# A softmax with a relative position bias: another assignment of row blocks to partitions

## The chip, the cores and the metric

The kernel runs on one core of one Trainium2 chip. The metric is the time of one execution on the device in microseconds, median of the runs shown. Beside it stands a profile of one execution, with its own time and its span, which is the time from the first to the last instruction of the core.

## What is computed

`logits` has the shape 2 x 8 x 2112 x 2112 (batch, head, row, column) in float32, `rel_bias` 8 x 33. Each row gets a bias that depends only on head and on row minus column, clipped to -16..16, and is then put through a softmax:

```
rel = pos[:, None] - pos[None, :]
rel_clipped = np.clip(rel, -16, 16) + 16
logits = logits + rel_bias[:, rel_clipped][None]
logits = logits - logits.max(axis=-1, keepdims=True)
exp = np.exp(logits)
out = exp / exp.sum(axis=-1, keepdims=True)
```

The input and the output have 285.5 MB each; the output has the shape and type of `logits`.

## The kernel before

**Tiling.** There are 2 x 8 x 2112 = 33792 rows. They are cut into 128 blocks of RP = 264 neighbouring rows, and partition p holds block p, for the whole run. NB = 8 blocks make up one head of one batch, so the low three bits of p say which eighth of the 2112 rows the block is (q in the code), and the next three bits are the head (h). A block is walked in steps of R = 6 rows: one buffer `X[m]` holds 6 x 2112 float32, 50688 bytes, in each partition. There are NBUF = 4 buffers and K = 11 rounds over them, so 44 buffers in all.

**Data movement.** `rows` (line 71) gives the DRAM address pattern of one buffer: 128 runs of 50688 bytes, one for each partition, RP * S elements apart. `load` (line 88) issues it from SyncE (SP) and `store` (line 91) from ScalarE (ACT); each is one DMA of 6336 KB. Four loads are issued at the start; after that, SP waits for the store of buffer m (the wait is in `take`, line 86) and issues the load of the next round into it.

**Work on a buffer.** For each of the six rows of a buffer, VectorE (DVE) adds the bias to the logits, negates and takes the minimum in one custom instruction (`add`, line 184), then ACT takes exp with that minimum as its bias and sums the row (`exps`, line 195). When all six are done, DVE takes the reciprocals (line 208) and scales four of the rows (line 211); ACT scales the other two (line 216) and issues the store (line 93). The order on each engine is written out by hand, in two loops, one on DVE and one on ACT, and semaphores join them. An `add` waits for its load by the semaphore `ld[m]`, again in `take` at line 86, as all the waits do that also lower a semaphore.

**Setup.** Before the loops, each partition builds the vector `F` of the bias that its block of rows sees, from its own q and h. Pool writes the partition's number into `pid` (line 124). DVE cuts q and h out of it with an and and a shift (lines 131 and 132), copies both as floats into `qh` in PSUM (line 135), and compares them with 0, 1, 2 ... (line 140). A small DMA from ACT's queue (line 120) brings the table of biases; line 142 is the first that needs it. `settle` is a wait of DVE for its own earlier instructions. The loop copies the part of `F` that a round needs into `F2` (line 170).

```
def rows(t, k, m):
    return bass.AP(
        tensor=t.tensor, offset=t.offset + m * R * S + k * (G * S), ap=[[RP * S, P], [1, R * S]],
    )
```

Of the kernel before, what the change touches and what calls it, by code (L numbers as in the profile page):

```python
# [8 lines left out]
I32 = mybir.dt.int32  # L9
ACTF = mybir.ActivationFunctionType  # L10
ALU = mybir.AluOpType
# [4 lines left out]
def kernel(  # L16
# [6 lines left out]
    nc = tc.nc  # L23
    P = 128
    B, H, S, S2 = logits.shape
# [3 lines left out]
    RP = B * H * S // P  # L29
# [5 lines left out]
    R = 6  # L35
    G = NBUF * R
# [5 lines left out]
    io = ctx.enter_context(tc.tile_pool(name="io", bufs=1))  # L42
    X = [io.tile([P, R * S], FP32, tag=f"X{b}", name=f"X{b}") for b in range(NBUF)]
    F2 = io.tile([P, SW + 1], FP32, tag="F2", name="F2")
    pid = io.tile([P, 2], I32, tag="pid", name="pid")
    own = io.tile([P, W + 2 * NB + 1], FP32, tag="own", name="own")
    rbK, rest, reg = own[:, 0:W], own[:, W : W + NB], own[:, W + NB : W + 2 * NB + 1]
    nmax = io.tile([P, NBUF * R], FP32, tag="nmax", name="nmax")
# [8 lines left out]
    def small(n):  # L57
        zc[0] += 16 * -(-n // 16)
        return Z[:, zc[0] - 16 * -(-n // 16) : zc[0] - 16 * -(-n // 16) + n]

    eq, lt, hsel = (small(NB) for _ in range(3))
    le, gt = (small(NB + 1) for _ in range(2))
    qh = small(2)

    def view(t, offset, dims):
        return bass.AP(tensor=t.tensor, offset=t.offset + offset, ap=[[list(t.ap[0])[0], P]] + dims)

    def rows(t, k, m):
        return bass.AP(
            tensor=t.tensor, offset=t.offset + m * R * S + k * (G * S), ap=[[RP * S, P], [1, R * S]],  # L70
        )

    with tc.tile_critical(no_gpsimd_drain=True):  # L73
# [8 lines left out]
        idx = nc.alloc_semaphore("idx")  # L82
        dve = nc.alloc_semaphore("dve")

        def take(eng, sem, n):
            eng.wait_ge(sem, n).then_inc(sem, -n)  # L86

        def load(k, m):
            nc.sync.dma_start(out=X[m][:, :], in_=rows(logits, k, m)).then_inc(ld[m], 16)

        def store(k, m):
            take(nc.scalar, scaled, R)
            nc.scalar.dma_start(out=rows(out, k, m), in_=X[m][:, :]).then_inc(st[m], 16)
# [10 lines left out]
        v = nc.vector  # L104
        done = [0]

        def then(ins):
            done[0] += 1
            ins.then_inc(dve, 1)

        def settle():
            take(v, dve, done[0])
            done[0] = 0
# [7 lines left out]
            out=bass.AP(tensor=F2.tensor, offset=F2.offset, ap=[[Q * step, P // Q], [1, H * W]]),  # L121
            in_=bass.AP(tensor=rel_bias.tensor, offset=rel_bias.offset, ap=[[0, P // Q], [1, H * W]]),
        ).then_inc(rb, 16)
        nc.gpsimd.iota(pid[:, :], pattern=[[0, 2]], base=0, channel_multiplier=1).then_inc(idx, 1)
        nc.gpsimd.iota(
            num, pattern=[[1, NB + 1]], base=0, channel_multiplier=0,
            allow_small_or_imprecise_dtypes=True,
        ).then_inc(idx, 1)

        v.wait_ge(idx, 2)  # L130
        then(v.tensor_scalar(out=pid[:, 0:1], in0=pid[:, 0:1], scalar1=NB - 1, scalar2=None, op0=ALU.bitwise_and))
        then(v.tensor_scalar(out=pid[:, 1:2], in0=pid[:, 1:2], scalar1=3, scalar2=H - 1,
                             op0=ALU.logical_shift_right, op1=ALU.bitwise_and))
        settle()
        then(v.tensor_copy(out=qh, in_=pid[:, :]))
        settle()
        q, h = qh[:, 0:1], qh[:, 1:2]
        for o, n, s, op in ((eq, NB, q, ALU.is_equal), (lt, NB, q, ALU.is_lt), (hsel, NB, h, ALU.is_equal),
# [24 lines left out]
                           in_=view(reg, 1, [[1, NB - 1], [0, RP - W]])))  # L163
# [97 lines left out]
```

## Time and profile before

| what | value |
|---|---|
| median of 3 runs | 1325.65 us (1325.03 to 1326.21) |
| the profiled execution, its own time | 1327.36 us |
| its span | 1325.6 us |
| bytes read and written in HBM | 285.48 MB and 285.47 MB |
| mean rate of the DMA engines | 431 GB/s |
| DVE busy | 866.1 us |
| ACT busy | 757.2 us |
| load, issue to landing, median | 39.0 us |
| store, issue to landing, median | 58.8 us |

The profile has one line for each group of instructions: line of the kernel, engine, operation, tiles written and read, shape and count; then the busy time in us and the mean of one in ns; then the idle time of the engine just before these instructions and what ended it. "DVEq L86" is DVE's own queue at the wait in line 86. In the queue lines, q1 carries the loads from SP, q10 the stores (and the table of biases) from ACT, and the last number is the time of its packets as a share of 16 engines over the span. In the line of tenths, each digit is the busy share of one fortieth of the span.

### The profile page before, as it was taken

How to read it: one execution, taken by the hardware profiler on the slowest of the kernel's cores; microseconds unless marked ns; L12 is line 12 of the kernel's file. 1: busy time of each engine (PE TensorE's matmuls, PEld its weight loads, DVE VectorE, ACT ScalarE, POOL GpSimd, SP SyncE). 2: the span in 40 equal slices, each digit the busy share in tenths (PEclk: the TensorE clock that was granted, in tenths of full speed). 3: DMA queues.
4: the chain of work that ended last, by engine and by line, in shares of the span. 5: the costliest groups of instructions: out<-in, count | busy, mean ns of one | idle time of the engine just before them, and what ended most of it. 6: DMA issues, size and time to landing. Idle time of an engine off the chain costs nothing. (4 is left out here: it accounts for less than half of the span.)

```text
span 1325.6 us, 2109 instructions
## 1 busy us (share of the span) xinstructions
DVE 866.1 (65%) x781; ACT 757.2 (57%) x627; POOL 0.4 (0%) x6
## 2 busy tenths in 40 slices
DVE  6886656566766675566667566556766676566663
ACT  3776555556665565555556565555665665555563
POOL 0000000000000000000000000000000000000000
DMA  9999999999999999999999999999999999999998
GB/s 416 416 433 424 441 428 428 441 424 433 441 428 431 436 425 433 439 430 434 434 430 433 437 434 425 437 434 434 428 439 436 422 441 434 431 431 436 428 433 389
DMA packets 12682, 570.98 MB, mean 431 GB/s; under 512 B 1412, under 2 KB 1416, under 8 KB 1416
## 3 DMA queue, kind: packets, MB, share of 16 engines
q1 hardware_dynamic: 6336, 285.48, 50.1%
q10 hardware_dynamic: 6344, 285.48, 49.8%
q14 instruction: 2, 0.02, 0.0%
HBM read 285.48 MB, written 285.47 MB: 431 GB/s over the span
## 5 line engine op out<-in xcount | busy, mean ns | idle before, releaser
L195 ACT ACTIVATE X<-X,nmax 128x2112 f32<-128x2112 f32 x264 | 542.6, 2055 | 508.0 <-DVE nmax L184 475.3
L184 DVE CUSTOM_DVE_ANT_0 X<-X,F 128x2112 f32<-128x2112 f32 x264 | 605.2, 2354 | 322.3 <-DVEq L86 322.3
L211 DVE TENSOR_SCALAR X<-X,rec 128x2112 f32<-128x2112 f32 x176 | 220.3, 1315 | 2.8
L216 ACT ACTIVATE X<-X,rec 128x2112 f32<-128x2112 f32 x88 | 176.1, 2048 | 17.2 <-DVE rec L208 12.2
L208 DVE RECIPROCAL rec<-tot 128x6 f32<-128x6 f32 x44 | 8.4, 191 | 106.2 <-DVEq L86 106.2
L195 ACT ACTIVATION_READ_ACCUMULATOR X<-X,nmax 128x1 f32 x264 | 49.2, 186 | 0.0
L195 ACT ACT_TABLE_LOAD x11 | 14.1, 1283 | 22.6 <-ACTq L86 19.9
L170 DVE COPY F<-F 128x2135 f32 x11 | 26.1, 2373 | 0.5 <-DVEq L86 0.5
L184 DVE DVE_READ_ACCUMULATOR2_ANT nmax<- 128x1 f32 x264 | 21.7, 82 | 0.0
L142 DVE LOAD_MASK_SELECT F<-F x1 | 0.0, 14 | 6.0 <-DMA F<-in_rel_bias_dram 6.0
L162 DVE COPY F<-own 128x1617 f32<-128x1617 f32 x1 | 1.8, 1835 | 0.0
L118 DVE MEMSET F<- 128x264 f32 x1 | 0.3, 278 | 1.1 <-SPq L73 1.1
L140 DVE TENSOR_SCALAR Z<-rec,Z 128x8 f32<-128x8 f32 (+1 forms) x5 | 0.8, 227 | 0.1
L148 DVE TENSOR_REDUCE own<-F 128x33 f32<-128x264 f32 x1 | 0.6, 608 | 0.1
L161 DVE TENSOR_TENSOR F<-F,own 128x264 f32<-128x264 f32 x1 | 0.4, 442 | 0.1
L145 DVE TENSOR_TENSOR F<-F,Z 128x264 f32<-128x264 f32 x1 | 0.4, 428 | 0.1
L142 DVE STREAM_SHUFFLE F<-F 128x264 f32<-128x264 f32 x1 | 0.4, 443 | 0.0
L158 DVE TENSOR_TENSOR F<-Z,own 128x264 f32<-128x264 f32 x1 | 0.4, 432 | 0.0
L166 DVE COPY F<-own 128x247 f32<-128x247 f32 x1 | 0.4, 410 | 0.0
L164 DVE COPY F<-own 128x247 f32<-128x247 f32 x1 | 0.4, 408 | 0.0
L156 DVE SCALAR_TENSOR_TENSOR own<-Z,own 128x8 f32<-128x8 f32 x1 | 0.2, 227 | 0.2 <-DVEq L86 0.2
L153 DVE TENSOR_SCALAR own<-Z,own 128x8 f32<-128x8 f32 x1 | 0.2, 226 | 0.1
(11 smaller groups left out, 1.6 us busy)
## 6 DMA issues: line engine op xcount, KB each, us to landing
X<-in_logits_dram SPq DMA_DIRECT2D x44, 6336.0 KB, 39.0
out_dram<-X ACTq DMA_DIRECT2D x44, 6336.0 KB, 58.8
F<-in_rel_bias_dram ACTq DMA_DIRECT2D x1, 4.1 KB
```

Of the source, the lines that this page charges most:

```text
L140: then(v.tensor_scalar(out=o, in0=num[:, 0:n], scalar1=s, scalar2=None, op0=op))
L142: then(v.stream_shuffle(out=T, in_=T, mask=[0] * Q))
L145: then(v.tensor_tensor(out=heads, in0=view(F2, 0, [[W, H], [1, W]]), in1=view(hsel, 0, [[1, H], [0, W]]), op=ALU.mult))
L148: then(v.tensor_reduce(out=rbK, in_=view(F2, H * W, [[1, W], [W, H]]), axis=mybir.AxisListType.X, op=ALU.add))
L158: then(v.tensor_tensor(out=bands, in0=view(eq, 0, [[1, NB], [0, W]]), in1=view(rbK, W - 1, [[0, NB], [-1, W]]), op=ALU.mult))
L162: then(v.tensor_copy(out=view(F, C0 + W, [[RP, NB - 1], [1, RP - W]]), in_=view(reg, 1, [[1, NB - 1], [0, RP - W]])))
L170: then(v.tensor_copy(out=F2[:, 0:SW], in_=F[:, bass.ds(RP - G - k * G, SW)]))
L184: v.tensor_tensor_reduce(out=row(m, i), in0=row(m, i), in1=F2[:, x : x + S], scale=-1.0, scalar=BIG, op0=ALU.add, op1=ALU.min, accum_out=c ...
L195: nc.scalar.activation(out=row(m, i), in_=row(m, i), func=ACTF.Exp, scale=-1.0, bias=col(nmax, m, i), accum_out=col(tot, m, i),).then_inc( ...
L208: v.reciprocal(out=col(rec, m, 0, R), in_=col(tot, m, 0, R)).then_inc(inv, 1 if m < NBUF - 1 else NBUF + 1)
L211: v.tensor_scalar_mul(out=row(m, i), in0=row(m, i), scalar1=col(rec, m, i)).then_inc(scaled, 1)
L216: nc.scalar.activation(out=row(m, i), in_=row(m, i), func=ACTF.Copy, scale=col(rec, m, i),).then_inc(scaled, 1)
```

## The change

Partition p = 8e + j (e from 0 to 15, j from 0 to 7) holds block 16j + e in place of block 8e + j. The DRAM side of each load and store is written with two outer dimensions in place of one: 16 steps of one block, and in each of them 8 steps of 16 blocks. The order of the partitions in SBUF, the size of each run, the number of DMAs and both loops are unchanged.

Since a block's eighth and head follow from its number, the setup finds them in another way. With b = 16j + e, the eighth is q = e mod 8, which is (p >> 3) and 7, and the head is (b >> 3) mod 8 = (2j + (e >> 3)) mod 8, that is 2 (p and 3) + (p >> 6). `pid` gets a third column for it, and the sum is made in floats by one more instruction.

```
-    pid = io.tile([P, 2], I32, tag="pid", name="pid")
+    pid = io.tile([P, 3], I32, tag="pid", name="pid")
...
-    qh = small(2)
+    qh, qs = small(2), small(1)
...
+    E = 16
+
     def rows(t, k, m):
         return bass.AP(
-            tensor=t.tensor, offset=t.offset + m * R * S + k * (G * S), ap=[[RP * S, P], [1, R * S]],
+            tensor=t.tensor, offset=t.offset + m * R * S + k * (G * S),
+            ap=[[RP * S, E], [E * RP * S, P // E], [1, R * S]],
         )
...
-        nc.gpsimd.iota(pid[:, :], pattern=[[0, 2]], base=0, channel_multiplier=1).then_inc(idx, 1)
+        nc.gpsimd.iota(pid[:, :], pattern=[[0, 3]], base=0, channel_multiplier=1).then_inc(idx, 1)
...
+        then(v.tensor_scalar(out=pid[:, 0:1], in0=pid[:, 0:1], scalar1=3, scalar2=None, op0=ALU.logical_shift_right))
+        then(v.tensor_scalar(out=pid[:, 1:2], in0=pid[:, 1:2], scalar1=3, scalar2=1,
+                             op0=ALU.bitwise_and, op1=ALU.logical_shift_left))
+        settle()
+        then(v.tensor_scalar(out=pid[:, 2:3], in0=pid[:, 0:1], scalar1=3, scalar2=None, op0=ALU.logical_shift_right))
         then(v.tensor_scalar(out=pid[:, 0:1], in0=pid[:, 0:1], scalar1=NB - 1, scalar2=None, op0=ALU.bitwise_and))
-        then(v.tensor_scalar(out=pid[:, 1:2], in0=pid[:, 1:2], scalar1=3, scalar2=H - 1,
-                             op0=ALU.logical_shift_right, op1=ALU.bitwise_and))
-        settle()
-        then(v.tensor_copy(out=qh, in_=pid[:, :]))
+        settle()
+        then(v.tensor_copy(out=qh, in_=pid[:, 0:2]))
+        then(v.tensor_copy(out=qs, in_=pid[:, 2:3]))
+        settle()
+        then(v.tensor_scalar(out=qh[:, 1:2], in0=qh[:, 1:2], scalar1=qs, scalar2=None, op0=ALU.add))
         settle()
```

## Prediction

> **What bounds the kernel now.** I read the summary page first: the busy times, the DMA lines and the queues.
>
> ```profile
> span 1325.6 us, 2109 instructions
> ...
> DVE 866.1 (65%) x781; ACT 757.2 (57%) x627; POOL 0.4 (0%) x6
> ...
> DMA  9999999999999999999999999999999999999998
> GB/s 416 416 433 424 441 428 428 441 424 433 441 428 431 436 425 433 439 430 434 434 430 433 437 434 425 437 434 434 428 439 436 422 441 434 431 431 436 428 433 389
> DMA packets 12682, 570.98 MB, mean 431 GB/s; under 512 B 1412, under 2 KB 1416, under 8 KB 1416
> ...
> q1 hardware_dynamic: 6336, 285.48, 50.1%
> q10 hardware_dynamic: 6344, 285.48, 49.8%
> q14 instruction: 2, 0.02, 0.0%
> ```
>
> No compute engine is near full, while the DMA line is at nines throughout. The two queues together hold 50.1 + 49.8 = 99.9% of the time of the 16 DMA engines, so there is hardly a gap between two transfers on any engine. The packets are long: 12682 less 1416 small ones and 2 instruction fetches are 11264, which is 44 x 128 on each queue, one row of six rows of logits (6 x 2112 x 4 = 50688 bytes) for each partition. Each engine therefore carries 704 of them, 352 from each queue. A load packet takes 0.501 x 1325.6 / 352 = 1.887 us, a store packet 0.498 x 1325.6 / 352 = 1.875 us (completion writes included). So the time of this kernel is one number, **704 packets at 1.881 us on each engine, 1324.3 us**, plus 1.3 us around it. The profiled execution took 1327.36 us, 1.76 more than its span; the median shown, 1325.65, lies 1.71 below that, so that a time worked out for the span is also one for the median.
>
> Next I ask whether the compute engines could become the bound, from the groups of instructions.
>
> ```profile
> L195 ACT ACTIVATE X<-X,nmax 128x2112 f32<-128x2112 f32 x264 | 542.6, 2055 | 508.0 <-DVE nmax L184 475.3
> L184 DVE CUSTOM_DVE_ANT_0 X<-X,F 128x2112 f32<-128x2112 f32 x264 | 605.2, 2354 | 322.3 <-DVEq L86 322.3
> ```
>
> DVE idles 322.3 us at the wait of line 86, the one on the load's semaphore. That is the idle time that a late load causes; over 44 buffers it is 7.3 us for each. Slower DMA goes straight into the time, and faster DMA would have some 7 us of room in each 30.1 us (1324.3 / 44) before DVE became the bound.
>
> Then the stages, since a mean over the span could hide one: loads alone at the start, loads and stores in turn, stores alone at the end. Columns are the stretch, its length, the busy times, the clock, the DMA share and GB/s.
>
> ```profile
> 0.00:18.00 18.00, 9.11 (x23) 1.28 (x1) 0.43 (x6) 1.00 0.96 397
> 18.00:40.00 22.00, 18.88 (x17) 16.89 (x14) 0.00 (x0) 1.00 0.95 412
> ...
> 120.00:600.00 480.00, 312.08 (x275) 275.04 (x228) 0.00 (x0) 1.00 1.00 432
> 600.00:1200.00 600.00, 391.38 (x348) 344.75 (x287) 0.00 (x0) 1.00 1.00 433
> ...
> 1300.00:1325.60 25.60, 5.20 (x5) 4.56 (x4) 0.00 (x0) 1.00 0.86 374
> ```
>
> With loads alone the rate (412) is within 5% of that with both kinds (432 and 433). The packets take the same 1.88 us whether an engine's neighbours read or write. So in this kernel the 16 engines **never slow one another**: not in memory, and not where they enter the 128 partitions. The views of one line's DMAs give the same from the other side: the fastest load and the fastest store, the ones that run by themselves.
>
> ```profile
> DMA to landing us min/median/max: 17.5/39.0/82.6
> ```
>
> ```profile
> DMA to landing us min/median/max: 18.2/58.8/59.5
> ```
>
> Eight packets of 1.88 us are 15.0 us, so a lone load (17.5) and a lone store (18.2) have about 3 us of start and completion beside them.
>
> **The change part by part.** There are two parts: the setup on DVE and Pool that finds each partition's head and block, and the address pattern of the 88 large DMAs.
>
> *Setup.* The old chain on pid, from the timeline (start, length):
>
> ```profile
> 1.30 0.15 DVE L131 TENSOR_SCALAR pid<-pid 128x1 int32<-128x1 int32 x1
> 1.38 0.14 DVE L132 TENSOR_SCALAR pid<-pid 128x1 int32<-128x1 int32 x1
> 1.67 0.16 DVE L135 CAST Z<-pid 128x2 f32<-128x2 int32 x1
> 1.98 0.77 DVE L140 TENSOR_SCALAR Z<-rec,Z 128x8 f32<-128x8 f32 x5
> 8.74 0.01 DVE L142 LOAD_MASK_SELECT F<-F  x1 [5.99 <-DMA F<-in_rel_bias_dram]
> ```
>
> The change makes seven small instructions of these first three and adds two waits for DVE's own semaphore: four instructions at 0.16 us and two gaps of about 0.15 us (1.52 to 1.67 is one), 0.9 us. The iota of 3 columns in place of 2 adds nanoseconds. Behind it, line 142 waits 5.99 us for the bias table; the 0.9 us lie wholly inside. If that cover were gone, they would go into the first add, once: 0.9 us of 1325. I take 0. Everything after line 142 is unchanged in number and size, in both loops too.
>
> *The pattern.* Bytes, packet size and number of DMAs stay (128 runs of 50688 bytes, 44 loads, 44 stores). What moves is which block a partition holds, and the form in which the DRAM side is written: one dimension of 128 becomes 16 by 8. Two costs hang on this.
>
> The issue itself: SP and ACT write one instruction for each DMA; a second dimension may make each dearer.
>
> ```profile
> L89 SPq DMA_DIRECT2D X<-in_logits_dram x44: 332/333/631, 1.0 to 1246.0; - x44
> ...
> L93 ACTq DMA_DIRECT2D out_dram<-X x44: 338/338/380, 40.3 to 1306.3; - x44
> ```
>
> At 0.33 us each, even doubling them costs ACT 0.34 us per buffer, beside 475.3 / 44 = 10.8 us in which it waits for DVE. Behind the store on ACT's queue stand the next buffer's exps, which wait for DVE anyway. SP only waits for stores. I take 0; at the two ends, where nothing covers it, it is at most 0.63 us.
>
> The dealing out: 128 partitions are dealt to 16 engines, and before shows a dealing in which no two engines meet. The diff replaces it. [...] Nothing in the trace shows what this new dealing does, so its price is bounded from both sides. Below: the loads lose what they take longer than stores, 50.1 - 49.8 = 0.3% of 1325.6, **4.0 us**; a packet faster than a store's 1.875 us is seen nowhere, so no gain beyond. Above: if the engines meet in pairs at the same partitions' entrance, both at half rate, a packet takes 3.76 us, and the sum is 1325.6 + c x 1324.3, where c is the share of the work that an engine does while its mate is at the same place. c = 0 gives 1326, c = 1 gives 2650.
>
> [...]
>
> Which c? One instruction hands all 16 engines their rows at one moment and in one order, so mates are in step, and every DMA waits for the slowest of the 16, so a pair that runs ahead is stopped at the next semaphore. That speaks for the high end. Against it: loads and stores alternate on each engine, so a mate that is one packet off writes while the other reads, and if the two directions don't disturb each other this costs nothing. I take c between 0.5 (only one direction meets, 1988 us) and 1 (2650 us), the middle, 0.75: 1325.6 + 993.2 = **2320 us**, nearer to the upper end because nothing in the loop brings mates out of step.
>
> **The rivals.**
>
> *Forecast, slower by meeting in pairs:* 2320, with 1500 (c = 0.13) to 2680 (c = 1 and one buffer's 30.1 us exposed) as its own bounds.
>
> *No effect:* the order in which blocks are visited doesn't matter, because 99.9% of the engines' time is streaming at one rate; or the change doesn't do what it says, and the chip deals the 16 by 8 pattern as before. For it: the flat rate in all stages. Against: then the dealing would have to be blind to the form. 1325.7 us.
>
> *Faster:* loads lose their 4.0 us because neighbouring blocks suit the memory better: 1321.6 us (-0.3%). For it: loads take 1.887 to the stores' 1.875 us, so there is something to lose. Against: part of this is the cold first load (397 GB/s in the first 18 us), which stays, and the engines must not meet. It decides only if more than 2.7 of the 4.0 us go and no pair meets.
>
> *Slightly slower by memory:* the 16 streams, now one block (264 x 2112 x 4 = 2.23 MB) apart, meet in DRAM. The lowest rate of a full slice on the page is 416 against 431: 431/416 x 1325.6 = 1373 us. It decides once the memory gives less than the engines' 431 GB/s; against it, no stage shows memory as a limit.
>
> **How the numbers follow.** Chances: forecast 0.78, slightly slower 0.06, no effect 0.10, faster 0.06. The rows weigh so because the gain is capped at 0.3% by a full DMA line, while the loss has no such cap and the one thing that keeps it away, the dealing without meetings, is what the diff rewrites. [...] About 0.2% (2.7 us) is what a measurement of this kernel can tell from no change. Faster by more than that: 0.06. Within: 0.10. Slower: 0.78 + 0.06 = 0.84. The range takes in the forecast's bounds and reaches down to the slight loss, 1370 to 2680; what is left out is no effect, faster, and a sliver beyond the bounds, together 0.2.
>
> **What would show it.** In the changed kernel's page, the packets (12682) and MB should be the same and the queues' shares still near 100% together, but with about 246 GB/s (571 MB / 2320 us) and packets of 3.3 us. The lone load and the lone store are the sharpest test: 17.5 and 18.2 us become 25 to 33 if mates meet, and stay if not. DVE's wait at the load's semaphore should grow from 7.3 us a buffer to about 30; DVE's and ACT's busy times stay at 866 and 757. If the load-only stage is slow and the mixed one is not, mates are out of step and c is near 0; if only loads are slow, one direction meets. I am wrong if the lone load lands in 17 to 18 us: then engines don't meet, and the time is within 4 us of 1325.

## The result, and the profile after

The changed kernel takes 1789.28 us, median of 6 runs (1746.99 to 1858.69), where the kernel before took 1325.86 us (1325.03 to 1328.78). The ratio is 1.326, 95% interval 1.317 to 1.334; like every ratio below it is formed from the runs within 1.5% of a kernel's fastest, here 1746.99, 1756.65 and 1770.57 us, so that it lies below 1789.28 / 1325.86 = 1.350. The runs of before lie within 0.3% of each other, those of the changed kernel are spread over 6%; that spread comes back below. The profiled execution took 1770.57 us, and its span is 1768.8.

From the summary page of the changed kernel, the lines that answer to those shown of before:

```profile
span 1768.8 us, 2115 instructions
...
DVE 866.9 (49%) x785; ACT 757.2 (43%) x627; POOL 0.4 (0%) x6
...
DMA  9999999999999999999999999999999999999997
GB/s 202 267 314 318 355 324 354 347 358 352 355 338 353 328 350 342 338 338 335 330 356 338 319 326 323 322 318 315 316 327 309 328 350 332 322 326 337 346 240 164
DMA packets 12682, 570.98 MB, mean 323 GB/s; under 512 B 1412, under 2 KB 1416, under 8 KB 1416
...
q1 hardware_dynamic: 6336, 285.48, 56.8%
q10 hardware_dynamic: 6344, 285.48, 42.5%
...
L193 DVE CUSTOM_DVE_ANT_0 X<-X,F 128x2112 f32<-128x2112 f32 x264 | 605.2, 2355 | 743.0 <-DVEq L89 743.0
...
L151 DVE LOAD_MASK_SELECT F<-F x1 | 0.0, 14 | 11.5 <-DMA F<-in_rel_bias_dram 11.5
```

Packets, bytes and compute times are those of before, and the DMA engines are as full as before: 56.8 + 42.5 = 99.3%. Each packet only takes longer, by its share of the span and its count, 352 on each engine and queue. A load packet takes 0.568 x 1768.8 / 352 = 2.854 us (before 1.887), a store packet 0.425 x 1768.8 / 352 = 2.136 us (before 1.875). The sums, 352 x 0.967 = 340 us and 352 x 0.261 = 92 us, are 432 of the 443 us by which the span grew; the rest is mostly time without a packet (0.7% of the span). DVE's wait at the load's semaphore grew from 322.3 to 743.0 us, and the setup still hides behind the bias table (line 151 waits 11.5 us).

Next the lone transfers. The issue of loads is line 92 now, that of stores line 96; the smallest number is the first load and the last store, the ones that run by themselves:

```profile
DMA to landing us min/median/max: 34.1/77.6/152.8
```

```profile
DMA to landing us min/median/max: 33.7/57.2/63.8
```

Both have about doubled, from 17.5 and 18.2. The stages of the changed kernel (stretch, length, busy times, clock, DMA share, GB/s) show that this doubling isn't kept up:

```profile
4.00:56.00 52.00, 26.00 (x31) 16.89 (x14) 0.00 (x0) 1.00 0.98 203
66.00:110.00 44.00, 18.96 (x17) 16.89 (x14) 0.00 (x0) 1.00 1.01 309
160.00:700.00 540.00, 282.30 (x251) 248.71 (x209) 0.00 (x0) 1.00 1.00 346
700.00:1600.00 900.00, 439.41 (x388) 387.39 (x320) 0.00 (x0) 1.00 1.00 329
...
1730.00:1766.00 36.00, 3.67 (x3) 2.65 (x2) 0.00 (x0) 1.00 0.86 186
```

With loads alone (first row) and stores alone (last row) the engines move half of what they moved in those stages of before, 412 and 374 GB/s. With both, they start at 309 and go on at 346 and 329, against 432 and 433. So the loss is nearly whole where one direction runs, and about a quarter where both alternate, which is most of the run.

### The profile page after: what moved, and what is told of

It is laid out like the page before. It is cut to its first block, busy times and chain, and to the rows that moved or that the text cites. A ratio compares the mean times of both kernels' runs of the same rounds, so it can differ in the third digit from the quotient of the medians.

```text
span 1768.8 us, 2115 instructions
## 1 busy us (share of the span) xinstructions
DVE 866.9 (49%) x785; ACT 757.2 (43%) x627; POOL 0.4 (0%) x6
## 3 DMA queue, kind: packets, MB, share of 16 engines
q1 hardware_dynamic: 6336, 285.48, 56.8%
q10 hardware_dynamic: 6344, 285.48, 42.5%
## 5 line engine op out<-in xcount | busy, mean ns | idle before, releaser
L193 DVE CUSTOM_DVE_ANT_0 X<-X,F 128x2112 f32<-128x2112 f32 x264 | 605.2, 2355 | 743.0 <-DVEq L89 743.0
L151 DVE LOAD_MASK_SELECT F<-F x1 | 0.0, 14 | 11.5 <-DMA F<-in_rel_bias_dram 11.5
## 6 DMA issues: line engine op xcount, KB each, us to landing
X<-in_logits_dram SPq DMA_DIRECT2D x44, 6336.0 KB, 77.6
```

The lines of the kernel that those rows point to most:

```text
L151: then(v.stream_shuffle(out=T, in_=T, mask=[0] * Q))
L193: v.tensor_tensor_reduce(out=row(m, i), in0=row(m, i), in1=F2[:, x : x + S], scale=-1.0, scalar=BIG, op0=ALU.add, op1=ALU.min, accum_out=c ...
```

## The experiments

Two questions had to be told apart: what is slow (the order of the blocks in memory, the form of the pattern, or the dealing of partitions to engines), and why it costs 443 us and not the 993 of the forecast. By "mates" I mean two engines that by my theory hinder each other because of the partitions they serve at the time; no record names them. "In step" means that they are at the same point of their work at the same time.

**Form alone, and each direction alone** (e1, e2, e3). The blocks stay in before's order. 64 elements less in the outer step keep the two dimensions from being merged into one of 128.

```
+    def rows2(t, k, m):
+        return bass.AP(
+            tensor=t.tensor, offset=t.offset + m * R * S + k * (G * S),
+            ap=[[P // E * RP * S - 64, E], [RP * S, P // E], [1, R * S]],
+        )
...
-            nc.sync.dma_start(out=X[m][:, :], in_=rows(logits, k, m)).then_inc(ld[m], 16)
+            nc.sync.dma_start(out=X[m][:, :], in_=rows2(logits, k, m)).then_inc(ld[m], 16)
...
-            nc.scalar.dma_start(out=rows(out, k, m), in_=X[m][:, :]).then_inc(st[m], 16)
+            nc.scalar.dma_start(out=rows2(out, k, m), in_=X[m][:, :]).then_inc(st[m], 16)
```

e1 has both edits, e2 that of the loads, e3 that of the stores.

> The blocks stay where they were before (partition p holds block p, each group of eight moved by at most 3840 bytes so that the two dimensions can't be merged); only the form, 16 by 8, of both address patterns is the changed kernel's. The output is therefore not the reference's (blocks are shifted by up to 960 elements, the bias is not). Theory (dealing): the form decides which engine serves which partitions, engines then meet in pairs at the partitions; about as the changed kernel, 1790 us (1740 to 1860), lone load 34 us. Rival (memory order): neighbouring blocks in DRAM collide; the order here is that of before, so 1326 us and a lone load of 17.5 us.

> As e1, but only the loads have the 16 by 8 form; stores are as before. Theory (dealing, directions separate, an engine reads for one packet while it writes another): a meeting in one direction alone already sets the pace; in step a load and a store together take 3 packet times in place of 2, so at most 1326 x 1.5 = 1989 us, and 1650 to 1900 if mates drift apart as in the changed kernel. Rival (costs of loads and stores add up): the changed kernel's loads take 56.8% of its time and its stores 42.5%, 1005 and 752 us against 664 and 660 before, so +341 us, 1667 us. Rival (memory order): 1326 us.

> As e1, but only the stores have the 16 by 8 form; loads are as before. The output is not the reference's (blocks are written up to 960 elements early). Theory (dealing, reading and writing of an engine overlap): same as e2, 1650 to 1989 us, with a lone load of 17.5 and a lone store of 34 us. Rival (costs add up, by the queue shares of the changed kernel): stores cost 752 - 660 = 92 us, so 1418 us. Rival (memory order): 1326 us.

Measured: e1 1771.51 us (1738.72 to 1868.32), e2 1645.13 (1634.82 to 1670.74), e3 1608.46 (1562.77 to 1617.41), before on the same chip 1325.59. The queue lines of the three pages, e1 first:

```profile
span 1773.8 us, 2109 instructions
...
q1 hardware_dynamic: 6336, 285.48, 56.4%
q10 hardware_dynamic: 6344, 285.48, 42.9%
```

```profile
span 1669.0 us, 2109 instructions
...
q1 hardware_dynamic: 6336, 285.48, 57.6%
q10 hardware_dynamic: 6344, 285.48, 41.3%
```

```profile
span 1612.5 us, 2109 instructions
...
q10 hardware_dynamic: 6344, 285.48, 50.8%
q1 hardware_dynamic: 6336, 285.48, 45.9%
```

e1 has the changed kernel's time without its order: memory order is not the cause, the form of the pattern is. The two directions don't add up: 319.5 us for the loads and 282.9 for the stores are 602, but both together cost 446. So e3 is a miss for the rival of adding costs (1418). e2 alone doesn't tell the theories apart, as its 1645 us lies within 1.4% of that rival's 1667 too. e2 and e3 end at or a little below the lower end of my theory's range: one direction costs less than one extra packet time (1.88 us) for each load and store, 319.5 / 352 = 0.91 us in e2 and 282.9 / 352 = 0.80 us in e3.

**Dealing without the form** (e5). The form is flat, but a transfer is cut into two halves of the partitions.

```
-            nc.sync.dma_start(out=X[m][:, :], in_=rows(logits, k, m)).then_inc(ld[m], 16)
+            for a in (0, P // 2):
+                nc.sync.dma_start(out=X[m][a : a + P // 2, :], in_=half(logits, k, m, a)).then_inc(ld[m], 16)
```

The store is cut in the same way, and the waits are for 32. `half` is `rows` with P // 2 runs from block a.

> Before's blocks and its one-dimensional form, but each load and store is issued as two DMAs, partitions 0 to 63 and 64 to 127; output as the reference. Theory (dealing: what counts is how many groups of partitions are visited at a time): 16 engines on one half of the partitions meet in pairs, so a lone load (its two halves) takes about 32 us and the whole 1700 to 2000 us. Rival (the two-dimensional form itself is dear): the form is flat here, so 1326 to 1335 us, lone halves at 9 to 10 us each.

Measured: 1804.41 us (1766.45 to 1825.0), ratio 1.342 (1.332 to 1.352). Its page:

```profile
GB/s 208 271 326 328 325 323 351 357 354 340 328 331 336 320 324 302 312 312 311 316 306 315 311 309 327 307 317 332 330 311 314 318 321 344 325 316 326 309 298 173
DMA packets 14091, 570.98 MB, mean 315 GB/s; under 512 B 2821, under 2 KB 2825, under 8 KB 2825
```

The first slice, loads alone, is at 208 GB/s as in the changed kernel. No half of a transfer lands before 17.6 us, where the rival had 9 to 10. A flat pattern over half of the partitions gives the same picture, so it isn't the second dimension as such that is dear. Nor is it the cutting into several DMAs, which costs 0.34% in e6 below. What is left, by exclusion, is which partitions the 16 engines have open at one time: with half of the partitions the load-only slice has half of the rate, 208 of before's 412 GB/s.

**The dose** (e9). Eight transfers of 16 neighbouring partitions for each buffer: the same loop as in e5 with `for a in range(0, P, 16)`, and waits for 128.

> Before's blocks in flat form, output as the reference, but each load and store as eight DMAs of 16 neighbouring partitions, one row for each engine. Theory (what counts is how many groups of partitions are open at one time): four engines share one place, a load packet takes 7.5 us, the first load (8 parts) lands after 60 us or so and the whole takes 2200 to 3300 us. Rival (pairs are the worst case, or it is the two-dimensional form): 1326 to 1810 us.

Measured: 1950.95 us (1886.68 to 2015.22, two runs). The stages of e9:

```profile
4.00:60.00 56.00, 7.75 (x14) 0.00 (x0) 0.00 (x0) 1.00 1.02 116
60.00:110.00 50.00, 18.97 (x17) 16.89 (x14) 0.00 (x0) 1.00 0.93 134
110.00:300.00 190.00, 61.63 (x55) 52.00 (x44) 0.00 (x0) 1.00 1.00 225
300.00:600.00 300.00, 113.61 (x101) 102.58 (x85) 0.00 (x0) 1.00 1.00 256
600.00:1000.00 400.00, 196.49 (x173) 171.43 (x142) 0.00 (x0) 1.00 1.00 317
1000.00:1700.00 700.00, 331.53 (x293) 293.54 (x243) 0.00 (x0) 1.00 1.00 322
```

The start is as the theory has it, 116 GB/s being near a quarter of before's 433 (108), and the fastest of these transfers lands after 9.2 us, about one packet of four times 1.88 us and its start. But the time is far below the expected 2200 to 3300. In the first row there are loads alone, and in the second the stores only begin. From the third row on loads and stores alternate by the same instructions, and yet the rate climbs from 225 and 256 to 317 and 322 GB/s, near the 329 to 346 of the changed kernel. Nothing in the program changes along these four rows. What can change is where the engines stand relative to each other; a count of this stands at the end of this section.

**Neighbouring blocks without the new form** (e4, e6). e4 keeps before's flat form; e6 keeps the output too.

```
-            tensor=t.tensor, offset=t.offset + m * R * S + k * (G * S), ap=[[RP * S, P], [1, R * S]],
+            tensor=t.tensor, offset=t.offset + m * (P * K * R * S) + k * (R * S), ap=[[K * R * S, P], [1, R * S]],
```

That is e4: the runs of two neighbouring partitions lie 66 rows apart in DRAM in place of 264. In e6, partition 4i + r holds block 32r + i, and four DMAs replace one (waits for 64, q and h found accordingly):

```
+            for r in range(Q4):
+                nc.sync.dma_start(out=parts(m, r), in_=rows(logits, k, m, r)).then_inc(ld[m], 16)
...
+            tensor=X[m].tensor, offset=X[m].offset + r * w, ap=[[Q4 * w, P // Q4], [1, R * S]],
```

> [...] The bias is that of before's blocks, so the output is not the reference's. Theory (only the dealing counts): 1326 us within 3. Rival (neighbouring blocks suit the memory): loads lose their 4 us, 1322. Rival (they collide in memory): 1373 or more, towards the changed kernel's 1790.

> Neighbouring blocks, output as the reference: partition 4i+r holds block 32r+i, and each load and store is issued as four DMAs, one for each r, of every fourth partition, in flat form of 32, so that the engines of one such DMA spread over all partitions. Theory (dealing): no pair meets, 1326 us, plus at most 44 x 2 x 3 more completions of some tens of ns on each engine, 1326 to 1335 us. Rival (neighbouring blocks in DRAM, or many DMAs, are at fault): 1600 to 1800 us.

Measured: e4 1325.74 us, ratio 1.0000 (0.9991 to 1.0009); e6 1330.27 us, ratio 1.0034 (1.0021 to 1.0046). The queue lines of e4 and of e6:

```profile
q1 hardware_dynamic: 6336, 285.48, 49.9%
q10 hardware_dynamic: 6344, 285.48, 49.8%
```

```profile
DMA packets 16907, 571.00 MB, mean 429 GB/s; under 512 B 5636, under 2 KB 5640, under 8 KB 5640
...
q1 hardware_dynamic: 8448, 285.49, 50.1%
q10 hardware_dynamic: 8456, 285.49, 49.7%
```

Runs that lie closer together (e4) and neighbouring blocks in each DMA (e6) neither help nor hurt by 1%. Loads take 49.9% in e4 against 50.1%, but no time is gained. e6 pays 0.34%, 4.5 us, beside 4224 more small packets; that is 264 for each of the 16 engines, and some 17 ns for each. This is the version that does what the change is called after without its price; neither it nor e4 beats the kernel before.

**Load and store by themselves and together** (e10). The loops are replaced by series such as this one, the fourth of four:

```
+        for k in range(5):
+            nc.sync.dma_start(out=X[0][:, :], in_=grid(logits, k, 3)).then_inc(ld, 16)
+            nc.scalar.dma_start(out=grid(out, k, 3), in_=X[1][:, :]).then_inc(st[n[0] % 2], 16)
+            both()
```

> No softmax: only transfers of one buffer's size, each started when the DMA engines are empty, five of each kind; flat is before's form and order, grid the changed kernel's. Lone flat load and store: 17 to 18 us. Lone grid load and store: 33 to 35 us by the dealing, 17 to 18 if form and order are harmless. Then a load and a store started together; both have landed after: flat with flat 33 us (16 packets of 1.88 us and 3). Theory (mates stay in step, but an engine reads for one packet while it writes another): 3 packet times for each load and store, 48 us, whether loads, stores or both are grid. Rival (mates in step, no such overlap): 48 us with one of them grid, 63 with both. Rival (mates are out of step within a few packets): 35 to 42 us in all three.

Issue to landing in us, median of five:

| load | store | load landed | store landed |
|---|---|---|---|
| flat | none | 17.7 | |
| grid | none | 33.9 | |
| none | flat | | 16.4 |
| none | grid | | 32.8 |
| flat | flat | 38.4 | 38.6 |
| grid | flat | 46.9 | 43.3 |
| flat | grid | 34.1 | 36.2 |
| grid | grid | 44.5 | 46.4 |

The rows of e10 for the lone grid load, and for the store of the last series:

```profile
L92 SPq DMA_DIRECT2D X<-in_logits_dram x5: 536/537/647, 107.6 to 243.6; - x5
...
DMA to landing us min/median/max: 33.6/33.9/34.1
```

```profile
L114 ACTq DMA_DIRECT2D out_dram<-X x5: 555/555/557, 1136.6 to 1323.0; - x5
...
DMA to landing us min/median/max: 46.1/46.4/46.7
```

Alone, either direction takes double (33.9 against 17.7 us, 32.8 against 16.4). Together, both grid take 46.4 us, no more than with a grid load and a flat store (46.9), and far from 63. A grid store beside a flat load costs nothing at all (36.2, less even than flat with flat, for which I have no reason). So in these pairs only the loads pay. The packet records of the last series add to it: in its first repetition the 16 engines' load packets take 3.56 us on average for the first of eight, 3.95 for the second, then 3.40, 3.33, 3.22, 3.13, 3.10 and 3.08; store packets stay at 1.95 to 2.07.

**One direction for the whole run** (e7). The changed kernel with stores cut short.

```
-            nc.scalar.dma_start(out=rows(out, k, m), in_=X[m][:, :]).then_inc(st[m], 16)
+            nc.scalar.dma_start(out=first(out, k, m), in_=X[m][:, 0:128]).then_inc(st[m], 16)
```

> The changed kernel, but a store writes only 128 of the 12672 columns of each partition (512 bytes), so that nearly all traffic is loads; all the rest of the work is done. Theory (a lag of a packet or less helps only where loads and stores alternate): with one direction mates meet on all of the way, 205 to 225 GB/s from begin to end, 1300 to 1420 us. Rival (mates drift apart in any traffic): the rate rises through the run as in the changed kernel, and the time falls to 1000 to 1250 us; without any meeting DVE and ACT would set 44 x 21.3 us and ends, about 980.

Measured: 1400.88 us, one run. Its stages:

```profile
4.00:56.00 52.00, 26.14 (x31) 16.89 (x14) 0.00 (x0) 1.00 0.98 203
100.00:600.00 500.00, 314.41 (x279) 276.38 (x229) 0.00 (x0) 1.00 1.01 210
600.00:1300.00 700.00, 443.54 (x393) 393.25 (x328) 0.00 (x0) 1.00 1.01 211
```

The rate stays at 210 to the end. Half the rate is not a starting effect; with loads alone it never comes near before's 412. The changed kernel differs from this in its stores, and with them it moves 309 to 346 GB/s, so it is the alternation with them that relieves it.

**A head start** (e8). Ten extra loads ahead of the first one, six of 12 rows and four of 4 rows, meant to make some engines start on the loop's loads later than others. If a lag between engines helps, the load-only stage should move more than the changed kernel's 203 GB/s:

```
+        for n, step, b, c in ((12, 9, 3, 6), (4, 8, 2, 4)):
+            for i in range(c):
+                nc.sync.dma_start(
+                    out=bass.AP(tensor=X[b].tensor, offset=X[b].offset + (4 + i) * w, ap=[[step * w, n], [1, R * S]]),
+                    in_=bass.AP(tensor=logits.tensor, offset=logits.offset + i * R * S, ap=[[RP * S, n], [1, R * S]]),
+                ).then_inc(late, 16)
```

> [...] Output as the reference. [...]

Measured: 1720.27 us (1659.43 to 1747.1) with the ten extra transfers in it. Two stages of e8:

```profile
30.00:60.00 30.00, 4.09 (x3) 1.69 (x1) 0.00 (x0) 1.00 1.07 270
66.00:110.00 44.00, 27.84 (x26) 26.48 (x22) 0.00 (x0) 1.00 0.99 330
```

The load-only stage (first row) moves 270 GB/s, above 203 but short of before's 412, and the runs take 1659 to 1747 us where those of the changed kernel take 1747 to 1859. The ten extra issues took until 8.3 us. The records don't name engines, so no lag was seen. The rate of the load-only stage speaks for a lag that helps; it doesn't measure how large the lag was, or how much a larger one would help.

**How many engines load at one time.** The packet records of the changed kernel's profile give each packet's queue, start and length. They don't name its engine, but how many of the 16 engines have a load packet open at a moment can be counted. The second column is the share of the time in which at most 3 or at least 13 have one, that is, in which nearly all go the same way:

| stretch, us | nearly all the same way | load packet, us | store packet, us | GB/s |
|---|---|---|---|---|
| 66 to 110 | 56% | 3.29 | 2.03 | 309 |
| 160 to 700 | 8% | 2.61 | 2.08 | 346 |
| 700 to 1600 | 14% | 2.90 | 2.04 | 329 |

The same packets (66 to 1600 us), sorted by how many other engines go the same way, on average over the packet's first 1.8 us:

| others | under 4 | 4 to 6 | 6 to 8 | 8 to 10 | 10 to 12 | 12 and more |
|---|---|---|---|---|---|---|
| load packet, us | 2.05 | 2.27 | 2.42 | 2.86 | 3.15 | 3.47 |
| store packet, us | 2.08 | 2.06 | 2.05 | 2.03 | 2.07 | 1.93 |

The first class of loads and the last of stores have only 45 and 43 packets. In the kernel before, load and store packets take 1.87 to 1.88 us in every one of these classes, so being in step is not dear in itself. In the changed kernel the engines are in step when the stores begin and then come out of step, and a load packet is the longer, the more others load beside it. (This is a correlation: long packets are also more often open together.) A store pays some 0.2 us, whatever the count. From 65.9 to 68.7 us all 16 engines store at once; the two packets of each take 2.04 and 1.87 us on average, where the 215 stores that start after the last load packet take 3.68. What spares the stores is thus not the lag.

## Why the prediction was wrong, point by point

- **The bound and the cause were right.** The kernel is 704 packets on each engine, before and after. The dealing sets their price, by exclusion, as the records don't name engines: e1 has the loss without the new order, e4, with runs 66 rows apart, and e6, with neighbouring blocks in each DMA, are without the loss (1.0000 and 1.0034), e5 has the loss with flat patterns. Setup and issue cost nothing that shows, though the issue of a load went from 0.33 to 0.54 us (line 92 of e10, above).
- **The test by lone transfers was right**: 34.1 and 33.7 us, at the upper end of the 25 to 33 I named, slightly beyond. There c is about 1. The other signs came out about half as strong as forecast: DVE's wait is 743.0 / 44 = 16.9 us a buffer (about 30), a packet takes 2.5 us on average (3.3), and the rate is 323 GB/s (246).
- **No run shows that engines meet in pairs, both at half rate**, on which the 3.76 us of the sum rest: the records don't name engines. What the runs show is the rate: with loads alone 203 GB/s in place of 412, with stores alone 186 in place of 374, with both 309 to 346 in place of 432.
- **The step that failed is "I take c between 0.5 ... and 1, the middle, 0.75"**, with its reason "nothing in the loop brings mates out of step". (In step they begin: the first load packets of the 16 engines start at 2.65 to 3.26 us in the changed kernel.) From the profiled spans, c = (1768.8 - 1325.6) / 1324.3 = 0.33. By direction, loads lost 0.967 of 1.887 us, 0.51, and stores 0.261 of 1.875, 0.14; their mean is the 0.33. Two things were mis-sized.
 First, stores: I let both directions meet at the upper end. In alternation stores hardly pay: e10's pair costs 46.4 us with both grid and 46.9 with the load alone, and a grid store beside flat loads nothing. They pay as little where all 16 engines store in step (2.04 and 1.87 us). That takes the upper end from 1 to about 0.5. Of the 92 us of the stores, 24 are packets that start after the last load packet, where stores are alone; the others take 2.07 us.
 Second, loads: even they don't meet all the time. The rate climbs from 309 to 346 GB/s in the changed kernel and from 225 to 322 in e9, under unchanged instructions; within one restarted buffer of e10 load packets fall from 3.95 to 3.08 us. The counts go with this: with 12 and more others loading a load packet takes 3.47 us, with fewer than 4 it takes 2.05, and the time in which nearly all go the same way falls from 56% to 8%. So something does bring engines out of step. My other reason, that a pair which runs ahead is stopped at the next semaphore, leaves out the queue: a load lands 77.6 us after its issue (median) and a buffer passes every 1768.8 / 44 = 40.2 us, so by this estimate about two loads are in the queue, and an engine that is ahead has work. The spread of the runs (1747 to 1859, against 0.3% before) fits a lag that chance sets, and e7, where there is nothing to alternate with, stays at 210. I called this the argument against and gave it too little.
- **What stays open.** The records don't name engines, so the counts show all 16 coming out of step, and the lag within a pair of mates is inferred. What starts the lag wasn't tested. Why stores pay so little next to loads isn't settled: a lone grid store takes double (32.8 us against 16.4), so stores can lose as much as loads. That an engine reads for its next packet while it still writes the last one would fit the 2.04 and 1.87 us of 16 stores in step, and would give e10's 46 us for both grid, but it would also give about 46 for flat loads with grid stores, where 36.2 was measured. And e3 over a whole run loses 283 us, more than e10's short series would say; by its queue lines a store packet there takes 2.33 us (159 us more in all), a load packet 2.10 (76 us), though loads are flat, and 3.3% of the span (53 us) has no packet.
- **The rivals.** No effect is refuted by the result. Faster and slower by memory order are refuted as causes by e4 and e6: runs 66 rows apart give 1.0000 (0.9991 to 1.0009), neighbouring blocks in each DMA 1.0034 (1.0021 to 1.0046).

## What to carry to other kernels

The way in which an address pattern is written can cost half of the DMA rate (203 of 412 GB/s with loads alone), as I read it because it decides which DMA engine serves which partitions; no record here names the engines. A pattern over 16 by 8, 64 or 16 partitions lost here (1789, 1804 and 1951 us), and a flat one over 128 (1326), or over every fourth partition (1330), didn't. Compare a transfer that runs by itself (its issue to landing) before and after such an edit: 17.5 against 34 us told the cause in one line. But price the loss from the stage that fills the run: in a full queue of loads and stores the factor of two came to 1.33.

## What was not expected of the hardware

Loads and stores that alternate partly undo a loss that halves the rate of either alone: 203 GB/s with loads, 186 with stores, and 309 to 346 with both. All 16 engines can store in step at about 2 us a packet (2.04 and 1.87) next to loads, where lone stores of the same form take 3.68. Transfers of 16 neighbouring partitions start at 116 GB/s, and yet settle at 317 to 322, near the 329 of the 16 by 8 form. A flat load and a flat store that start together on empty engines need 38.4 us, more than the 33 that their 16 packets of 1.88 us and 3 us of start and completion would make.
